# Reordered weight sums, later casts and value tiles transposed one at a time in a two-layer retention and convolution trunk

## The chip, the core and the metric

The kernel runs on one core of a Trainium2 chip. The core has TensorE (PE, matmuls, with PEld as its weight loads), VectorE (DVE), ScalarE (ACT), GpSimd (POOL) and SyncE (SP, which issues the DMAs here). Each engine takes its own instructions in the order of its own queue and waits for the others by semaphores. The metric is the device time of one execution in microseconds (us); it is given as the median of several runs, and one further execution was recorded by the profiler.

## The reference

A sequence of 528 tokens (16 learned ones and 512) with 1024 channels goes through two layers. A layer normalises its input, multiplies it by one large weight matrix, cuts the product into ten parts, and runs two branches on them:

```
xn = _rmsnorm(h, pre_norm_g[l])
proj = xn @ w_in[l] + b_in[l]
c_h, c_b, c_c, c_z, r_q, r_k, r_v, r_z, g_a, g_b = jnp.split(proj, split_at, axis=-1)
y_a = _short_conv_branch(c_h, c_b, c_c, c_z, conv_w[l], conv_b[l], w_conv_out[l])
y_b = _retention_branch(r_q, r_k, r_v, r_z, ret_gn_g[l], w_ret_out[l])
y = jax.nn.sigmoid(g_a) * y_a + jax.nn.sigmoid(g_b) * y_b
y = y @ w_o[l]
h = h + _rmsnorm(y, post_norm_g[l])
```

The convolution branch is a three-tap convolution over tokens of `c_c * c_h`, times `c_b` and `silu(c_z)`, times a weight matrix. The retention branch has 4 heads with 256 channels for q and k and 512 for v: q and k are rotated (rope), the scores q·k are weighted by a decay that is zero for keys of later chunks, the scores multiply v, each head's output is normalised over its 512 channels, multiplied by `silu(r_z)` and by a weight matrix. The chunkwise recurrence of the reference is computed here as one masked product per head. All is float32.

## The kernel before

**Matmuls in three products.** Every float32 operand is split into a high part (ACT's cast to float32r, L142) and a low part (DVE's subtraction, L143), by the helper `split`; a product is hi·hi + hi·lo + lo·hi, three matmuls. Weight pairs are called whi and wlo, and whd and wld for the fourth tile of a block; pairs of intermediate results are tiles of the ring r.

**Blocks of weights (`Group`).** A group is 256 output columns of the large matrix. It is computed by seven block products instead of eight, on sums of the input's blocks (A11 to S4 in Xh and Xl) and of the weight's blocks. Three raw weight tiles a, b, c of 128x1024 come by DMA into a ring of six (tag raw). DVE builds the weight sums in them: `halves(0)` adds the two halves of a and of c in place (L307, both here), then splits a; `sums` forms b's sum (L314) and t4 (L315) and splits b; `halves(2)` splits c; `last` splits t4. These four steps are queued by `prep` and carried out by `pump` whenever a pair of buffers comes free (four pairs, two single ones). A block product is one `mul`, 12 matmuls (four pieces of depth by three products) of up to 264 columns on PE (L279), followed by a `tick`. The results lie in PSUM banks pb (two), pc and pa (one each); `put` (L325, ACT) evicts them into SBUF slots with signs and biases, L335 copies one product into pa, and L356 (DVE) adds two results. `run` calls the callback cb of the group one block later.

**Side work (`later` and `tick`).** What follows from a block's result is not emitted at once: `later(delay, fn)` puts fn into a heap with the tick at which it is due, and `tick`, called after each `mul` and after every second step of the other matmul loops, runs what is due. So a delay is counted in block products of PE. The scheduler then places the instructions on each engine's queue; work under `tc.high_priority()` goes ahead of casts where both are ready.

**One retention head.** `k_done` and `q_done` call `rope`: two steps, each with two products (L403, L404), their sum or difference (L405) and a split into r tiles. `k8` (delay 3) copies a small piece of k twice. `scores` multiplies k and q (L422), DVE weights by the decay (L433), and a split writes Shi and Slo. `v_done` starts `vtrans`: the values, channel-major, are transposed on PE (L447) into token-major tiles, five key tiles of up to 128 keys (j = 0 to 4). Two of them share one `pslot`, a pp buffer of two PSUM banks; there are two pp buffers in all, which scores, attend, the statistics and the output products use too. For each key tile ACT writes the high part with the sum along the row (L454), then again with the mean taken off (L455; L459 for a piece of the last tile), and DVE writes the low part (L460). The sums `s` come from a ring of two (tag vs).

`z_done` runs when the gate z has arrived: silu on the second tile (L866), then `attend` for the four value pieces v = 0 to 3, two ticks apart: PE multiplies the scores by the values (L481) into the two banks of a pp (in layer 1 one bank); ACT squares a bank (L492), DVE multiplies the same bank by the norm's weight and the gate (L493), then the other bank in the same way; for v > 0 DVE adds the squares to `sums` (L496). `normed` follows: `stats` (L370 on PE reads `sums`), `wide` (a spread of the result), and `finish`, which multiplies by it (L514) and splits.

**Convolution and gates.** `conv_group` multiplies, convolves (L558, L562, L564) and gates (L568, L570, L574) in the callbacks of four groups; `gate_b` and `gate_a` apply the sigmoids. `RetOut` and `ConvOut` are the branch output products (L244 on PE), added into YB by L538 and L540.

**Opening.** The first head of each layer is computed by plain blocks (`Std`, L648) instead of groups, as the seven-product form needs sums of the input that aren't there yet; `with_r` (L992, L993) multiplies them by the token's norm, and L989 is their raw eviction.

Of the kernel before, what the change touches and what calls it, by code (L numbers as in the profile page):

```python
# [20 lines left out]
T = 528  # L21
# [35 lines left out]
def trunk(ctx: ExitStack, tc: tile.TileContext, xT, w_in, binT, w_co, w_ro, w_o, gpre, gpost,  # L57
# [226 lines left out]
    class Group:  # L284
        def __init__(self, l, col, i0, cb, act=AF.Identity):
            self.l, self.m, self.n, self.i0, self.cb, self.act = l, col // P, HALF - i0, i0, cb, act
            w = w_in[l, col // 256]
            need = [load(lambda j=j: self.load(j, w)) for j in range(3)][-1]
            prep("pair", need, 0, lambda: self.halves(0))
            prep("pair", need, 2, self.sums)  # L290
            prep("pair", need, 1, lambda: self.halves(2))
            prep("one", need, 0, self.last)
# [11 lines left out]
        def halves(self, j):  # L304
            if not j:
                for r in self.raw[0::2]:
                    nc.vector.tensor_tensor(r[:, 512:], r[:, 512:], r[:, 0:512], op=ALU.add)  # L307
            self.w[j] = wtile("whi"), wtile("wlo")
            split(*self.w[j], self.raw[j])
# [85 lines left out]
    def rope(tiles, t0):  # L395
# [5 lines left out]
        def step(u, v, op):  # L401
# [4 lines left out]
            hi, lo = rslot(), rslot()  # L406
            split(hi[:, cs], lo[:, cs], a[:, cs])
            res.append((hi, lo))
# [3 lines left out]
    def scores(l, q, k, k8, Shi, Slo, js):  # L412
# [14 lines left out]
        for n, j, cols in todo:  # L427
# [11 lines left out]
            split(Shi[0:kn, ss], Slo[0:kn, ss], sv)  # L439
# [23 lines left out]
    def attend(l, h, Shi, Slo, V, v, t, sums):  # L463
# [26 lines left out]
        with tc.high_priority():  # L490
            for b, (s0, s1) in enumerate(banks):
                nc.scalar.activation(sq[:, s0:s1], pp[:, b, 0:s1 - s0], AF.Square)  # L492
                nc.vector.scalar_tensor_tensor(t[:, s0:s1], pp[:, b, 0:s1 - s0], g, t[:, s0:s1], op0=ALU.mult, op1=ALU.mult)  # L493
# [6 lines left out]
    def normed(l, ts, sums, res):  # L500
# [11 lines left out]
        def finish(v):  # L512
            t = ts[v]
            nc.vector.tensor_tensor(t[:, cs], t[:, cs], st["rg"][:, cs], op=ALU.mult)  # L514
            hi, lo = rslot(), rslot()
            split(hi[:, cs], lo[:, cs], t[:, cs])
            res.append((hi, lo))
# [26 lines left out]
    def conv_group(l, i2, res):  # L544
# [7 lines left out]
        def c_c(ts):  # L552
            st["u"] = []
            for s in range(2):
                u = gr.tile([P, T + 2], F32, tag="u", name=nm("u"), bufs=2)
                if l < DEPTH - 1:
                    nc.vector.memset(u[:, 0:2], 0.0)
                nc.vector.tensor_tensor(u[:, 2 + cc.start:], ts[s][:, cc], st["h"][s][:, cc], op=ALU.mult)  # L558
                i = i2 * 2 + s
                a = ts[s]  # L560
                w = lambda j: cw_sb[:, l, j, i:i + 1]
                nc.scalar.activation(a[:, cs], u[:, 2 + cs.start:2 + T], AF.Identity, scale=w(2), bias=cb_sb[:, l, i:i + 1])  # L562
                for j in (1, 0):
                    nc.vector.scalar_tensor_tensor(a[:, cs], u[:, j + cs.start:j + T], w(j), a[:, cs], op0=ALU.mult, op1=ALU.add)  # L564
                st["u"].append(a)

        def c_z(ts):
            nc.scalar.activation(ts[1][:, cs], ts[1][:, cs], AF.Silu)  # L568
            for a, t in zip(st["u"], ts):
# [698 lines left out]
```

## Time and profile before

| | |
|---|---|
| median of 3 runs | 1588.45 us (1587.52 to 1591.75) |
| the profiled execution's own time | 1584.71 us |
| its span in the trace | 1582.9 us |
| PE busy | 1545.6 us, 98% |
| PEld busy | 1491.0 us, 94% |
| DVE busy | 1169.5 us, 74% |
| ACT busy | 909.7 us, 57% |
| POOL busy | 18.8 us, 1% |
| DMA moved | 174.37 MB, 110 GB/s on average |

The span is the time between the first and the last record of the trace. An engine is busy while it executes; waiting for a semaphore is idle time, which the trace ascribes to the instruction that came last of those waited for. The ends of matmuls are modelled, and matmuls overlap: a record lasts longer than the distance to the next one. PE and PEld run at the same time.

### The profile page before, as it was taken

The numbers are of one execution on the slowest core, as the hardware profiler recorded it, in microseconds if no ns is written. First come the engines' busy times: TensorE is split into PE (matmuls) and PEld (weight loads), VectorE is DVE, ScalarE is ACT, GpSimd is POOL, SyncE is SP. The second block draws the span as 40 slices with busy tenths as digits, with TensorE's granted clock in tenths as the row PEclk, the third lists the DMA queues.
The fourth block names the chain that finished last, engine by engine and source line by source line (L and its number), as shares of the span: only waits on it lengthen the run. The fifth ranks groups of instructions, "written<-read, shape, count | busy, mean of one in ns | idle before, by whom it ended". The sixth has DMA issues, their size and how long they took to land.

```text
span 1582.9 us, 29259 instructions
## 1 busy us (share of the span) xinstructions
PE 1545.6 (98%) x11762; PEld 1491.0 (94%) x11762; DVE 1169.5 (74%) x1702; ACT 909.7 (57%) x1763; POOL 18.8 (1%) x23
## 2 busy tenths in 40 slices
PE   9999999999999999999999999999999999999998
PEld 9988999999999999999999999999998999999986
DVE  6996776786877788867376878768869777997642
ACT  6584655555565466655354666665654655676531
POOL 0000000000000000000000000000000000000000
PEclk9999999999999999999999999999999999999999
DMA  8132322222232243335421223323232223334421
GB/s 266 61 114 71 116 101 94 94 101 87 101 107 94 89 139 127 126 129 187 122 102 48 101 86 115 114 94 114 94 107 101 94 88 131 130 130 141 144 94 53
DMA packets 86039, 174.37 MB, mean 110 GB/s; under 512 B 11280, under 2 KB 15888, under 8 KB 85904
## 3 DMA queue, kind: packets, MB, share of 16 engines
q1 hardware_dynamic: 85760, 172.50, 31.4%
q8 instruction: 92, 1.51, 0.4%
q14 instruction: 43, 0.35, 0.1%
q10 hardware_dynamic: 144, 0.01, 0.0%
HBM read 168.21 MB, written 4.26 MB: 109 GB/s over the span
## 4 chain that ended last, share of the span: by engine, by line
PE 81%; DVE 7%; ACT 6%; issue 3%; DMA 3%; SPq 0%; DVEq 0%; POOLq 0%; ACTq 0%
PE pb L279 26%; PE pp L244 16%; PE pc L279 13%; PE pp L648 7%; PE pa L279 7%; PE pp L481 4%; PE pp L1130 3%; PE pb L648 3%; DMA raw<-in_w_in 2%; DVE wlo L143 2%; ACT whi L142 2%; PE pp L422 2%; PE pp L384 1%; ACT r L454 1%; ACT r L455 1%
## 5 line engine op out<-in xcount | busy, mean ns | idle before, releaser
L143 DVE TENSOR_TENSOR wlo<-raw,whi 128x1024 fp32r<-128x1024 f32 (+2 forms) x358 | 392.9, 1107 | 140.7 <-ACT whi L142 138.3
L142 ACT CAST whi<-raw 128x1024 fp32r<-128x1024 f32 (+2 forms) x358 | 339.5, 958 | 235.1 <-PE pp L244 66.7
L279 PE MATMUL pb<-Xh,whi 128*128 128x264 f32 (+2 forms) x1008 | 289.4, 287 | 2.6 <-ACT pa L335 1.5
L279 PE MATMUL pb<-Xh,wlo 128*128 128x264 f32 (+2 forms) x1008 | 285.4, 283 | 0.1
L279 PE MATMUL pb<-Xl,whi 128*128 128x264 f32 (+2 forms) x1008 | 285.1, 283 | 0.0
L244 PE MATMUL pp<-r,whi 128*128 128x264 f32 (+1 forms) x1152 | 245.9, 321 | 0.0
L279 PE MATMUL pc<-Xh,whi 128*128 128x264 f32 (+2 forms) x672 | 193.7, 288 | 12.3 <-ACT f L325 12.2
L279 PEld LDWEIGHTS pb<-Xh,whi 128*128 128x128 f32 x1008 | 189.7, 188 | 4.8 <-ACT pa L335 2.1
L244 PEld LDWEIGHTS pp<-r,whi 128*128 128x128 f32 x1152 | 177.5, 188 | 15.9 <-ACT whi L142 0.5
L279 PE MATMUL pc<-Xl,whi 128*128 128x264 f32 (+2 forms) x672 | 191.0, 284 | 0.0
L279 PE MATMUL pc<-Xh,wlo 128*128 128x264 f32 (+2 forms) x672 | 190.7, 284 | 0.0
L279 PEld LDWEIGHTS pb<-Xl,whi 128*128 128x128 f32 x1008 | 189.7, 188 | 0.4
L279 PEld LDWEIGHTS pb<-Xh,wlo 128*128 128x128 f32 x1008 | 189.6, 188 | 0.4 <-DVE wlo L143 0.3
L244 PE MATMUL pp<-r,wlo 128*128 128x264 f32 (+1 forms) x576 | 152.8, 321 | 0.0
L307 DVE TENSOR_TENSOR raw<-raw 128x512 f32<-128x512 f32 x168 | 115.3, 686 | 43.6 <-DMA raw<-in_w_in 41.9
L279 PEld LDWEIGHTS pc<-Xh,whi 128*128 128x128 f32 x672 | 127.0, 189 | 16.3 <-ACT f L325 15.6
L279 PEld LDWEIGHTS pc<-Xl,whi 128*128 128x128 f32 x672 | 127.0, 189 | 0.2
L279 PEld LDWEIGHTS pc<-Xh,wlo 128*128 128x128 f32 x672 | 127.0, 189 | 0.1
L244 PEld LDWEIGHTS pp<-r,wlo 128*128 128x128 f32 x576 | 95.5, 188 | 8.0
L279 PE MATMUL pa<-Xh,whi 128*128 128x264 f32 (+2 forms) x336 | 96.7, 288 | 0.0
L279 PE MATMUL pb<-Xh,whd 128*128 128x264 f32 (+2 forms) x336 | 96.7, 288 | 0.0
L314 DVE TENSOR_TENSOR raw<-raw,raw 128x512 f32<-128x512 f32 x84 | 57.9, 689 | 51.8 <-DMA raw<-in_w_in 51.3
(219 smaller groups left out, 3329.6 us busy)
## 6 DMA issues: line engine op xcount, KB each, us to landing
raw<-in_w_in SPq DMA_DIRECT2D x426, 256.0 KB, 2.9
raw<-in_w_ro SPq DMA_DIRECT2D x32, 512.0 KB, 3.2
raw<-in_w_in SPq DMA_DIRECT2D x20, 512.0 KB, 5.0
raw<-in_w_co SPq DMA_DIRECT2D x16, 512.0 KB, 3.2
raw<-in_w_o SPq DMA_DIRECT2D x16, 512.0 KB, 3.6
Dsb<-in_decay SPq DMA_DIRECT2D x8, 520.0 KB, 4.7
h1d<-f SPq DMA_DIRECT2D x8, 264.0 KB, 4.4
f<-h1d SPq DMA_DIRECT2D x8, 264.0 KB, 4.3
```

The costliest lines, as they stand in the source:

```text
L142: nc.scalar.copy(dst_hi, src)
L143: nc.vector.tensor_tensor(dst_lo, src, dst_hi.bitcast(F32), op=ALU.subtract)
L244: nc.tensor.matmul(banks[i][:, 0:cols.n], wt(k)[:, msl], xs(k)[:, sl], start=(k == 0 and a == 0), stop=(k == nk - 1 and a == 2),)
L279: nc.tensor.matmul(o[:, 0:n], wt[:, k, :], xs[:, blk, k, HALF - n:], start=(first and k == 0 and a == 0), stop=(k == 3 and a == 2), skip_g ...
L307: nc.vector.tensor_tensor(r[:, 512:], r[:, 512:], r[:, 0:512], op=ALU.add)
L314: nc.vector.tensor_tensor(b[:, 0:512], a[:, 512:], c[:, 0:512], op=ALU.add)
L384: nc.tensor.matmul(pp[:, c // per, (c % per) * sc:(c % per + 1) * sc], y[:, c:c + 1].to_broadcast([sc, P]), ident[0:sc, 0:sc], start=True, ...
L422: nc.tensor.matmul(pp[0:kn, n + i, 0:cols.n], k[dt][x][:, k0:k0 + kn] if j < 4 else k8[:, dt * 2 + x, :], q[dt][y][:, sl], start=(dt == 0 ...
L454: nc.scalar.activation(hi[0:kn], pv, AF.Copy, scale=-1.0 / DV, accum_out=s)
L481: nc.tensor.matmul(pp[:, b, lo_ - banks[b][0]:hi_ - banks[b][0]], V[j][x][0:kn, v * P:(v + 1) * P], S[0:kn, SOFF[j] + lo_ - q0:SOFF[j] + h ...
L648: nc.tensor.matmul(o, wt(k), xs[:, i0:], start=(k == 0 and a == 0), stop=(k == KD - 1 and a == 2))
L1130: nc.tensor.matmul(o, x[:, xs], wo[k][half][w], start=(k == 0 and a == 0), stop=(k == KD - 1 and a == 2))
```

## The change

The instructions are the same and as many. Six things are emitted in another place:

- the sum in the third weight tile c (L307) is made in `halves(2)`, when c is split, and no longer in `halves(0)`; `halves(0)` now asks for the load of a alone;
- casts that follow products of DVE are put into `later`: those of `rope` by two ticks, those of `scores` and `finish` by one, `k8` from 3 to 5; `finish` itself begins at 14 in place of 15;
- the pieces of `conv_group`, and the silu and sigmoid of z and of the gates, are spread over zero to three ticks;
- in `attend` the squares of both banks come first, then both products;
- `vtrans` is called for one key tile at a time, every two ticks, and each has a pp buffer of its own (five in place of three per head);
- `v_done` starts three ticks earlier (34 to 31, 16 to 13, 12 to 9).

```
-            need = [load(lambda j=j: self.load(j, w)) for j in range(3)][-1]
-            prep("pair", need, 0, lambda: self.halves(0))
-            prep("pair", need, 2, self.sums)
-            prep("pair", need, 1, lambda: self.halves(2))
-            prep("one", need, 0, self.last)
+            need = [load(lambda j=j: self.load(j, w)) for j in (0, 1, 2)]
+            prep("pair", need[0], 0, lambda: self.halves(0))
+            prep("pair", need[2], 2, self.sums)
+            prep("pair", need[2], 1, lambda: self.halves(2))
+            prep("one", need[2], 0, self.last)
...
         def halves(self, j):
-            if not j:
-                for r in self.raw[0::2]:
-                    nc.vector.tensor_tensor(r[:, 512:], r[:, 512:], r[:, 0:512], op=ALU.add)
+            if j != 1:
+                r = self.raw[j]
+                nc.vector.tensor_tensor(r[:, 512:], r[:, 512:], r[:, 0:512], op=ALU.add)
...
             nc.vector.tensor_tensor(a[:, cs], a[:, cs], b[:, cs], op=op)
-            hi, lo = rslot(), rslot()
-            split(hi[:, cs], lo[:, cs], a[:, cs])
-            res.append((hi, lo))
+
+            def halves():
+                hi, lo = rslot(), rslot()
+                split(hi[:, cs], lo[:, cs], a[:, cs])
+                res.append((hi, lo))
+            later(2, halves)
...
-            split(Shi[0:kn, ss], Slo[0:kn, ss], sv)
+            later(1, lambda kn=kn, ss=ss, sv=sv: split(Shi[0:kn, ss], Slo[0:kn, ss], sv))
...
                 nc.scalar.activation(sq[:, s0:s1], pp[:, b, 0:s1 - s0], AF.Square)
+            for b, (s0, s1) in enumerate(banks):
                 nc.vector.scalar_tensor_tensor(t[:, s0:s1], pp[:, b, 0:s1 - s0], g, t[:, s0:s1], op0=ALU.mult, op1=ALU.mult)
...
             nc.vector.tensor_tensor(t[:, cs], t[:, cs], st["rg"][:, cs], op=ALU.mult)
-            hi, lo = rslot(), rslot()
-            split(hi[:, cs], lo[:, cs], t[:, cs])
-            res.append((hi, lo))
+
+            def halves():
+                hi, lo = rslot(), rslot()
+                split(hi[:, cs], lo[:, cs], t[:, cs])
+                res.append((hi, lo))
+            later(1, halves)
...
+            for s in range(2):
+                later(1 + s, lambda s=s: last_tap(s))
+                later(2 + s, lambda s=s: taps(s))
...
+            later(1, silu)
+            later(1, lambda: gate(0))
+            later(2, lambda: gate(1))
...
+            for s in range(2):
+                later(s, lambda s=s: product(s))
+                later(1 + s, lambda s=s: halves(s))
...
-            later(3, k8)
+            later(5, k8)
...
-                for n, js in enumerate(((0, 1), (2, 3), (4,))):
-                    later(d + 3 * n, lambda js=js: vtrans(vt, hd["v8"], V, js))
+                for j in range(len(JT)):
+                    later(d + 2 * j, lambda j=j: vtrans(vt, hd["v8"], V, (j,)))
...
-                nc.scalar.activation(ts[n][:, cs], ts[n][:, cs], AF.Silu)
+                later(1, lambda n=n: nc.scalar.activation(ts[n][:, cs], ts[n][:, cs], AF.Silu))
...
             for v in range(4):
-                later(15 + v, lambda v=v: hd["n"][2](v))
+                later(14 + v, lambda v=v: hd["n"][2](v))
...
-                add(Group(l, R_V + h * DV + n * 256, I_ALL[l], lambda ts, d=d: v_done(ts, d, 34)))
+                add(Group(l, R_V + h * DV + n * 256, I_ALL[l], lambda ts, d=d: v_done(ts, d, 31)))
...
-    v_done(vt, hd["hd"], 16)
+    v_done(vt, hd["hd"], 13)
...
-            v_done(opened[2:6], hd["hd"], 12)
+            v_done(opened[2:6], hd["hd"], 9)
```

The line numbers of the changed kernel differ: the value tile's steps L447, L454, L455, L459 and L460 are L450, L457, L458, L462 and L463 there, attend's L481, L492, L493 and L496 are L484, L495, L497 and L500, the decay's L433 is L436 and the add into YB is L547.

Below stand instructions in the order of one engine's queue; the numbers behind the tiles' names tell buffers apart and mean nothing else.

ACT before, in head 1 of layer 0, from the third value tile (L454 into r_2895) to the copy into pa (the tiles pp_2981 and pp_3049 hold the transposed values, pc_2930 and pb_2929 two block products, whi the casts of weights):

```order
L454 ACTIVATE r_2895,vs_2990<-pp_2981 128x512
L455 ACTIVATE r_2895<-pp_2981,vs_2990 128x512
L325 ACTIVATE f_2928<-pb_2929 128x264
L454 ACTIVATE r_2897,vs_2994<-pp_2981 128x512
L142 CAST whi_3026<-raw_2657 128x1024
L455 ACTIVATE r_2897<-pp_2981,vs_2994 128x512
L325 ACTIVATE f_2926<-pa_108 128x264
L454 ACTIVATE r_2899,vs_3054<-pp_3049 128x512
L142 CAST whi_3075<-raw_2798 128x1024
L455 ACTIVATE r_2899<-pp_3049,vs_3054 128x512
L459 ACTIVATE r_2900<-pp_3049,vs_3054 64x512
L325 ACTIVATE f_2927<-pc_2930,bin_92 128x264
```

ACT in the changed kernel at the same place, from the fourth value tile (pp_2992) on; pp_3028 holds the fifth, pc_2932 and pb_2931 the block products:

```order
L457 ACTIVATE r_2823,vs_2997<-pp_2992 128x512
L458 ACTIVATE r_2823<-pp_2992,vs_2997 128x512
L325 ACTIVATE f_2930<-pb_2931 128x264
L142 CAST whi_3040<-raw_2659 128x1024
L457 ACTIVATE r_2825,vs_3033<-pp_3028 128x512
L458 ACTIVATE r_2825<-pp_3028,vs_3033 128x512
L462 ACTIVATE r_2826<-pp_3028,vs_3033 64x512
L325 ACTIVATE f_2928<-pa_108 128x264
L325 ACTIVATE f_2929<-pc_2932,bin_92 128x264
L142 CAST whi_3078<-raw_2800 128x1024
L325 ACTIVATE f_2929<-pb_2931,bin_92 128x264
L335 ACTIVATE pa_108<-pb_3086,bin_92 128x264
```

Each value tile now has a pp of its own and its two or three ACT steps stand together; between the fifth tile's steps and the eviction of pc_2932 there is no cast of weights any more, and the next cast comes behind that eviction.

DVE before, at the beginning of the same head's transposed values (r_2892 is the low part of the first tile, r_2894 of the second):

```order
L314 TENSOR_TENSOR raw_2801<-raw_2798,raw_2859 128x512
L307 TENSOR_TENSOR raw_2859<-raw_2859 128x512
L143 TENSOR_TENSOR wlo_2922<-raw_2561,whi_2921 128x1024
L356 TENSOR_TENSOR f_2740<-f_2740,f_2741 128x528
L460 SCALAR_TENSOR_TENSOR r_2892<-pp_2901,vs_2910,r_2891 80x512
L143 TENSOR_TENSOR wlo_2961<-raw_2564,whi_2960 128x1024
L460 SCALAR_TENSOR_TENSOR r_2894<-pp_2901,vs_2914,r_2893 128x512
L143 TENSOR_TENSOR wld_3034<-t_2957,whd_3033 128x512
L307 TENSOR_TENSOR raw_2964<-raw_2964 128x512
L460 SCALAR_TENSOR_TENSOR r_2896<-pp_2981,vs_2990,r_2895 128x512
L315 TENSOR_TENSOR t_3111<-raw_2801 128x512
```

DVE in the changed kernel (r_2818 is the low part of the first tile, r_2820 of the second):

```order
L463 SCALAR_TENSOR_TENSOR r_2818<-pp_2827,vs_2832,r_2817 80x512
L143 TENSOR_TENSOR wlo_2873<-raw_2495,whi_2872 128x1024
L436 TENSOR_TENSOR f_2866<-pp_2853,Dsb 128x192
L436 TENSOR_TENSOR f_2868<-pp_2853,Dsb 128x64
L143 TENSOR_TENSOR Slo_2631<-f_2866,Shi_2630 128x192
L143 TENSOR_TENSOR Slo_2631<-f_2868,Shi_2630 128x64
L314 TENSOR_TENSOR raw_2803<-raw_2800,raw_2876 128x512
L307 TENSOR_TENSOR raw_2876<-raw_2876 128x512
L463 SCALAR_TENSOR_TENSOR r_2820<-pp_2895,vs_2900,r_2819 128x512
L143 TENSOR_TENSOR wlo_2924<-raw_2562,whi_2923 128x1024
L356 TENSOR_TENSOR f_2739<-f_2739,f_2740 128x528
```

The first tile's low part has moved from behind the weight sums L314 and L307 and a weight's low half to ahead of them; the second tile's stands behind the two sums in both.

DVE before, at a rope of k (f_3892 and f_3913 are its two results, r_3898 and r_3919 their low parts, YB the accumulated branch output):

```order
L403 TENSOR_TENSOR f_3892<-f_3757,cos_sb 128x528
L540 TENSOR_TENSOR YB<-pp_3879,YB 128x528
L404 TENSOR_TENSOR f_3893<-f_3758,sin_sb 128x528
L405 TENSOR_TENSOR f_3892<-f_3892,f_3893 128x528
L540 TENSOR_TENSOR YB<-pp_3923,YB 128x528
L143 TENSOR_TENSOR r_3898<-f_3892,r_3897 128x528
L143 TENSOR_TENSOR wlo_3953<-raw_3596,whi_3952 128x1024
L403 TENSOR_TENSOR f_3913<-f_3757,sin_sb 128x528
L540 TENSOR_TENSOR YB<-pp_3963,YB 128x528
L404 TENSOR_TENSOR f_3914<-f_3758,cos_sb 128x528
L405 TENSOR_TENSOR f_3913<-f_3913,f_3914 128x528
L314 TENSOR_TENSOR raw_3863<-raw_3860,raw_3956 128x512
```

DVE in the changed kernel (f_3895 and f_3912, r_3935 and r_3951):

```order
L403 TENSOR_TENSOR f_3895<-f_3761,cos_sb 128x528
L547 TENSOR_TENSOR YB<-pp_3882,YB 128x528
L404 TENSOR_TENSOR f_3896<-f_3762,sin_sb 128x528
L403 TENSOR_TENSOR f_3912<-f_3761,sin_sb 128x528
L405 TENSOR_TENSOR f_3895<-f_3895,f_3896 128x528
L404 TENSOR_TENSOR f_3913<-f_3762,cos_sb 128x528
L547 TENSOR_TENSOR YB<-pp_3918,YB 128x528
L405 TENSOR_TENSOR f_3912<-f_3912,f_3913 128x528
L143 TENSOR_TENSOR r_3935<-f_3895,r_3934 128x528
L143 TENSOR_TENSOR wlo_3957<-raw_3599,whi_3956 128x1024
L547 TENSOR_TENSOR YB<-pp_3967,YB 128x528
L143 TENSOR_TENSOR r_3951<-f_3912,r_3950 128x528
```

The products and sums of both steps now stand together, ahead of both low parts and of the weight's low half; the second sum has passed one add into YB and the low half wlo.

## Rows read from the trace of the kernel before

**Rows 1.** Page, part 1: busy time, share of the span, instructions of each engine.

```profile
PE 1545.6 (98%) x11762; PEld 1491.0 (94%) x11762; DVE 1169.5 (74%) x1702; ACT 909.7 (57%) x1763; POOL 18.8 (1%) x23
```

**Rows 2.** PE's waits, whole kernel: line and releaser, us in total, times, longest.

```profile
PE pc L279 <- ACT f L325: 12.2, 13, 1.6
PE pp L370 <- DVE f L496: 4.8, 3, 3.6
...
PE pp L481 <- DVE r L460: 1.6, 3, 0.7
PE pb L279 <- ACT pa L335: 1.5, 3, 0.6
...
PE pb L648 <- ACT f L989: 1.2, 1, 1.2
PE pb L279 <- ACT f L989: 1.1, 1, 1.1
```

**Rows 3.** Timeline, vtrans of head 1: start, duration, engine, line; in brackets idle before.

```profile
232.01 1.04 PE L447 MATMUL pp<-ident,f 128*80 128x128 f32 x8
233.74 0.69 DVE L314 TENSOR_TENSOR raw<-raw,raw 128x512 f32<-128x512 f32 x1 [1.73 <-DMA raw<-in_w_in]
235.23 0.69 DVE L307 TENSOR_TENSOR raw<-raw 128x512 f32<-128x512 f32 x1 [0.80 <-DMA raw<-in_w_in]
237.60 0.74 DVE L460 SCALAR_TENSOR_TENSOR r<-pp,vs,r 80x512 fp32r<-80x512 f32 x1
238.38 0.60 ACT L454 ACTIVATE r<-pp 128x512 fp32r<-128x512 f32 x1
...
248.34 0.68 ACT L459 ACTIVATE r<-pp,vs 64x512 fp32r<-64x512 f32 x1
248.90 0.48 ACT L325 ACTIVATE f<-pc,bin 128x264 f32<-128x264 f32 x1
249.44 0.40 PE L279 MATMUL pc<-Xh,whi 128*128 128x264 f32 x1 [1.02 <-ACT f L325]
249.67 0.28 PE L279 MATMUL pc<-Xl,whi 128*128 128x264 f32 x1
249.79 0.29 PE L279 MATMUL pc<-Xh,wlo 128*128 128x264 f32 x1
```

**Rows 4.** PE's waits in the stretch from 160 to 165 us.

```profile
PE pc L279 <- ACT f L325: 0.7, 1, 0.7
```

**Rows 5.** Busy us (instructions) of PE, PEld, DVE, ACT, POOL; granted clock; DMA share, GB/s.

```profile
141.00:147.70 6.70, 5.71 (x30) 5.74 (x31) 3.94 (x8) 3.19 (x7) 1.71 (x1) 0.50 0.11 39
...
250.00:253.60 3.60, 3.60 (x19) 3.60 (x18) 2.51 (x4) 1.67 (x4) 0.00 (x0) 0.53 0.48 151
253.60:258.00 4.40, 4.40 (x36) 4.32 (x35) 2.63 (x4) 1.99 (x5) 0.00 (x0) 1.00 0.32 119
```

**Rows 6.** Timeline, the last attend (v = 3) of head 0 in layer 0.

```profile
139.14 0.69 DVE L307 TENSOR_TENSOR raw<-raw 128x512 f32<-128x512 f32 x1 [1.66 <-DMA raw<-in_w_in]
...
140.21 0.44 ACT L492 ACTIVATE f<-pp 128x320 f32<-128x320 f32 x1 [3.23 <-DVE f L493]
...
140.68 0.55 DVE L493 SCALAR_TENSOR_TENSOR f<-pp,gn_sb,f 128x320 f32<-128x320 f32 x1 [0.51 <-ACT f L492]
...
141.99 0.42 PE L370 MATMUL pp<-ones_d,f 128*88 128x1 f32 x2 [3.65 <-DVE f L496]
```

**Rows 7.** Waits of ACT and DVE, whole kernel.

```profile
ACT f L492 <- DVE f L493: 24.2, 15, 3.9
...
DVE raw L314 <- DMA raw<-in_w_in: 51.3, 43, 2.6
DVE raw L307 <- DMA raw<-in_w_in: 41.9, 36, 3.6
```

**Rows 8.** Timeline, a rope of k and the scores behind it.

```profile
330.44 0.63 ACT L142 CAST r<-f 128x528 fp32r<-128x528 f32 x1 [3.94 <-DVE f L405]
...
333.21 0.71 PE L422 MATMUL pp<-r,r 128*80 128x264 f32 x4 [0.63 <-DVE r L143]
```

More of the change, by code (lines that the diff above doesn't have):

```diff
@@ L552, in c_c @@
         def c_c(ts):
-            st["u"] = []
+            st["u"] = [t for t in ts]
+            us = []
+            w = lambda s, j: cw_sb[:, l, j, i2 * 2 + s:i2 * 2 + s + 1]
             for s in range(2):
                 u = gr.tile([P, T + 2], F32, tag="u", name=nm("u"), bufs=2)
+                us.append(u)
                 if l < DEPTH - 1:
@@ L558, in c_c, with last_tap, taps @@
                 nc.vector.tensor_tensor(u[:, 2 + cc.start:], ts[s][:, cc], st["h"][s][:, cc], op=ALU.mult)
-                i = i2 * 2 + s
+            def last_tap(s):
+                nc.scalar.activation(ts[s][:, cs], us[s][:, 2 + cs.start:2 + T], AF.Identity, scale=w(s, 2),
+                                     bias=cb_sb[:, l, i2 * 2 + s:i2 * 2 + s + 1])
+            def taps(s):
                 a = ts[s]
-                w = lambda j: cw_sb[:, l, j, i:i + 1]
-                nc.scalar.activation(a[:, cs], u[:, 2 + cs.start:2 + T], AF.Identity, scale=w(2), bias=cb_sb[:, l, i:i + 1])
@@ L563, in c_c @@
                 for j in (1, 0):
-                    nc.vector.scalar_tensor_tensor(a[:, cs], u[:, j + cs.start:j + T], w(j), a[:, cs], op0=ALU.mult, op1=ALU.add)
-                st["u"].append(a)
-        def c_z(ts):
-            nc.scalar.activation(ts[1][:, cs], ts[1][:, cs], AF.Silu)
-            for a, t in zip(st["u"], ts):
-                nc.vector.tensor_tensor(a[:, cs], t[:, cs], a[:, cs], op=ALU.mult)
+                    nc.vector.scalar_tensor_tensor(a[:, cs], us[s][:, j + cs.start:j + T], w(s, j), a[:, cs],
+                                                   op0=ALU.mult, op1=ALU.add)
@@ new lines, in c_c, with silu, gate @@
+            for s in range(2):
+                later(1 + s, lambda s=s: last_tap(s))
+                later(2 + s, lambda s=s: taps(s))
+        def c_z(ts):
+            def silu():
+                nc.scalar.activation(ts[1][:, cs], ts[1][:, cs], AF.Silu)
+            def gate(s):
+                a = st["u"][s]
+                nc.vector.tensor_tensor(a[:, cs], ts[s][:, cs], a[:, cs], op=ALU.mult)
+            later(1, silu)
+            later(1, lambda: gate(0))
+            later(2, lambda: gate(1))
@@ L572, in c_b, with product, halves @@
         def c_b(ts):
-            for a, t in zip(st["u"], ts):
-                nc.vector.tensor_tensor(t[:, cs], t[:, cs], a[:, cs], op=ALU.mult)
+            def product(s):
+                nc.vector.tensor_tensor(ts[s][:, cs], ts[s][:, cs], st["u"][s][:, cs], op=ALU.mult)
+            def halves(s):
                 hi, lo = rslot(), rslot()
-                split(hi[:, cs], lo[:, cs], t[:, cs])
+                split(hi[:, cs], lo[:, cs], ts[s][:, cs])
                 res.append((hi, lo))
+            for s in range(2):
+                later(s, lambda s=s: product(s))
+                later(1 + s, lambda s=s: halves(s))
@@ L913, in gate_b, with sigmoid, times @@
             cs = slice(QCOLS[l].t0, T)
-            nc.scalar.activation(ts[1][:, cs], ts[1][:, cs], AF.Sigmoid)
-            for s, t in enumerate(ts):
+            def sigmoid():
+                nc.scalar.activation(ts[1][:, cs], ts[1][:, cs], AF.Sigmoid)
+            def times(s):
                 y = YB[:, b * 2 + s, cs]
-                nc.vector.tensor_tensor(y, y, t[:, cs], op=ALU.mult)
+                nc.vector.tensor_tensor(y, y, ts[s][:, cs], op=ALU.mult)
+            later(0, lambda: times(0))
+            later(1, sigmoid)
+            later(2, lambda: times(1))
         for b in range(4):
@@ L924, in gate_a @@
             cs = slice(QCOLS[l].t0, T)
-            nc.scalar.activation(ts[1][:, cs], ts[1][:, cs], AF.Sigmoid)
+            later(1, lambda: nc.scalar.activation(ts[1][:, cs], ts[1][:, cs], AF.Sigmoid))
             ga.extend(ts)
```

## Prediction

> **What bounds the kernel now.** I read the page's head first. TensorE (PE) is busy for 1545.6 of 1582.9 us, 98% [rows 1]; VectorE (DVE) has 74% and ScalarE (ACT) 57%. So DVE and ACT matter only where PE stands still for them, and everything that this change can give lies in PE's 37.3 us of idle time and in the stretches where its clock is low. No edit takes an instruction away; each only reorders.
>
> The second view is PE's list of waits [rows 2]: who ended PE's idle time, the total, how often, the longest. The reader is to see that one kind rules: matmuls into pc (bank c of the next block, its S1 product) wait for the eviction of pc on ACT (L325), 13 times, 12.2 us. Next is L370, the statistics matmul behind attend, for DVE's L496: 3 times, 4.8 us. Then L481 (attend) for L460 (the last step of a transposed value tile), 1.6 us; the pa copy L335, 1.5; two waits of the opening for L989, 1.2 and 1.1.
>
> A gap costs a little more than it shows. A matmul's record lasts 0.28 us, but the next one starts 0.12 us after it [rows 3], at 249.67 and 249.79, so each stop adds about 0.16 us to its gap.
>
> The third view is the timeline around single gaps: what stands in front of the late instruction on its own queue.
>
> **Where the pc waits come from: vtrans.** In [rows 3] two value tiles share one pp buffer. ACT's L454 for the second tile waits until DVE's L460 has read the first. DVE stood in front of DMA waits (1.73 us before L314 and 0.80 before L307), so L460 of the tile transposed at 232.01 ran only at 237.60, and ACT's next L454 at 238.38. All evictions queue behind it on ACT. Eight us later the same thing ends in PE's gap of 1.02 us at 249.44: L325 of pc runs at 248.90, behind a cast and the value steps, the last of them L459 at 248.34. Eleven of the thirteen pc waits are of this kind, by what stands on ACT in front of them; the other two, of which [rows 4] has one (0.7 us), follow finish's casts, in each layer one. So vtrans costs 12.2 − 1.4 + 1.6 = 12.4 us in 14 gaps (three of them L481's), and 14 × 0.16 = 2.2 on top: **14.6 us**.
>
> **The clock.** After 249.44 the granted clock is 0.53 for 3.60 us, in which 19 matmuls ran [rows 5]; at full clock 36 took 4.40 us, 0.122 each, so 19 need 2.3 and the dip cost 1.3 us. After the attend gap of 3.65 us it is 0.50: 30 matmuls in 5.71 us instead of 3.7, so **2.0 us** more.
>
> **The change part by part.**
>
> *One key tile per pp, earlier (vtrans).* Five pp buffers a head in place of three, same transposes, same ACT and DVE instructions. What goes is the wait of ACT for DVE inside a pp: the order shows each L457 waiting for its own transposes only. The last tile also comes three ticks earlier relative to the products that need it, a tick being one mul of 12 matmuls, 12 × 0.122 = 1.46 us, so L460's lateness at attend (0.7 us at the longest) [rows 2] is covered by more than four. And pc's eviction stands ahead of the whi cast that was before it. I take 13.0 of the 14.6, since some heads will still meet an eviction behind two value steps (L457 and L458 take 0.6 to 0.7 us each), and 1.0 of the 1.3 us of clock: **−14.0**. Bounds: 0, and −15.9.
>
> *Both squares ahead of both products (attend).* Before, the second bank's square waited for the first bank's product on DVE, and the second product for that square. In [rows 6], for v=3: L307 waits for its DMA until 139.14, product one follows it, square two comes only at 140.21 (ACT stood 3.23 us for the product), product two at 140.68 after 0.51 us, then L496, and PE goes on at 141.99. Over the kernel ACT's wait there is 24.2 us [rows 7]. After, DVE's 0.51 us is gone for each v. It adds up only where one v's products delay the next: here each of four v has such a step of about 0.5 us on DVE, and DVE's wlo between them sets free the raw buffer whose load the next L307 waits for. The chain would be 4 × 0.5 = 2.0 us earlier; I take 1.9. If the load does not follow, it is 0.5 to 1.0. The other two gaps on L370 are 4.8 − 3.6 = 1.2 us with 0.3 for their starts: about 1.4 in all, each under 0.85, which half a microsecond and an earlier chain should close: −1.4. The clock's 2.0 us at the first one go if the shorter gap keeps the clock up; I take half, −1.0. **−4.3**, between −0.5 and −7.3.
>
> [...] The rows show 0.50 after a gap of 3.65 us, and 0.53 after gaps of 0.7 and 1.02 us close together [rows 2, 3, 5, 6]. [...]
>
> *Rope's casts two ticks later, k8 at 5.* PE's L422 at 333.21 waits 0.63 us for DVE's cast of k, and ACT's cast at 330.44 stood 3.94 us for L405 [rows 8]. The order now has both rope products ahead of the casts and of an add into YB; with the third pa wait (1.5 − 2 × 0.6 = 0.3 us, at the pa copy behind the same casts) and the starts of both there is 1.3 us: **−1.3**, bounds 0 and that. Delaying a cast puts it nearer to the scores that read it; with L422 now behind both ropes, that is the price if I am wrong, up to the same 1.3.
>
> *The opening (with_r, ropes of head 0).* The two waits for L989 are 2.3 us [rows 2] and 0.3 for starting. Evictions stand further ahead on ACT there, yet PE has fewer pc muls to fill in: **−1.8**, bounds 0 and −2.6.
>
> *Finish's casts one tick later, begun one earlier.* The order around the gap of [rows 4] stays cast of whi, cast of r, eviction: **0**, bounds −3.3 (both pc gaps and two of L335 of 0.6, with starts) and +0.5 a head.
>
> *Conv and gate pieces, the z silu, the scores' casts.* No conv or gate line stands among PE's releasers [rows 2], so PE hides them; they cost nothing as long as PE's queue there has no wait. Same cost in instructions.
>
> *The weight sums.* L307 of the third weight tile moves from ahead of the first tile's cast to ahead of its own. DVE executes as many. L307 waits 41.9 us for DMA and L314 51.3 [rows 7]; the wait moves from the one to the other, because L314 reads that third tile in any case. What gains is the first tile's lo half, no longer queued behind the third tile's load; PE hardly ever waits for wlo, so **0**.
>
> *What the new order costs.* The order has 39 transposes that wait for a pp buffer instead of 24, and 19 evictions that wait for DVE to leave a slot instead of 9. The nearest rows are stops of PE of 0.16 us and up. 15 and 10 more at about 0.1 each: **+2.5**, between 0 and the slower rival's price.
>
> **Sum.** −14.0 − 4.3 − 1.3 − 1.8 + 2.5 = −18.9 us. The profiled execution took 1584.71 us, 3.74 under the median of 1588.45. So 1565.8 in its place, and about **1570 us** as a median.
>
> **Rivals.**
>
> *Half of it (DMA stays ahead on DVE).* DVE's 93 us of DMA waits [rows 7] stand in front of L463, L356 and L497 in the new order too. Then the ACT queue still waits for DVE, at the silu behind L356 for one, and half of each gain is lost: −7.0 − 2.1 − 0.7 − 0.9 + 1.0 = −9.7, **1578.7**. For it: in [rows 6] the load, not the square, sets 139.14. Against: in [rows 3] the tile's L460 stands behind L314 and L307, and the new order puts the first of them ahead.
>
> *The gaps only move.* The evictions stay behind other casts, and the gap of one product appears at the next: the change does not do what it says. −2 to 0, **1587**. Against: most gaps have free time behind them on ACT (57% busy).
>
> *Slower: pp buffers run out.* There are two pp buffers, and five tiles a head now pass through them, two muls (2.9 us) apart, so a buffer must be free 5.8 us after its transposes. In [rows 3] the first was transposed at 232.01 and let go at 238.34 (L460 of 0.74 us at 237.60): 6.3 us. If DVE lets go as late in the new order, PE stands at the transposes in place of pc, in order, with everything behind it. One DMA wait (up to 2.6 us [rows 7]) a head: 8 × 2.5 = 20 us, and vtrans gains nothing: 20 − 4.3 − 1.3 − 1.8 = +12.6, **1601**. It decides where the release passes 5.8 us; 0.5 us less and it costs nothing. Against: L463 of the first tile now precedes both waits.
>
> **Chances.** Forecast 0.60, half 0.24, moved 0.10, slower 0.06. About 0.3% (4.8 us) is what a measurement of this kernel can tell from no change. Faster than 1583.7: 0.60 + most of 0.24 = 0.82; within: 0.12; slower than 1593.2: 0.06. The range of 8 in 10 goes from 1561 (all gaps and clock gone, with half of the new costs) to 1584 (the half case with its own spread); left out are the moved and the slower case and a little at the fast end.
>
> **What would show it.** Right: pc's row for L325 falls from 12.2 to under 3 us, L481's row for L460 vanishes, ACT's wait for the product is gone, L370's row falls under 2.5, and the granted clock near 250 us stays at full. Half: the pc row between 4 and 9, with L463 or L356 behind L314 and L307. Moved: PE's idle time near 35 us under other names. Slower: a row of transposes (L450) that wait for L463, above 8 us. I should be wrong most easily in the new order's cost, which no row of before shows.

## The result, and the profile after

The changed kernel took 1564.61 us as a median (1560.22 to 1567.43, 4 runs) against 1588.12 us before: 23.5 us less, ratio 0.9845 with a 95% interval of 0.9817 to 0.9873. A second measurement, with the experiments below, gave 0.9832 (0.9811 to 0.9853). The forecast was 1570 with a range of 1561 to 1584: the time lies in the range, 5.4 us under the forecast. How the gain came about was only partly forecast: the largest term came out in size, but not by the cause that was given for it.

The page of the changed kernel's profiled execution, part 1 (before: [rows 1]):

```profile
span 1558.4 us, 29296 instructions
...
PE 1537.1 (99%) x11762; PEld 1487.0 (95%) x11762; DVE 1166.1 (75%) x1702; ACT 912.2 (59%) x1763; POOL 18.8 (1%) x23
```

PE's idle time is 21.3 us in place of 37.3, with as many matmuls. PE's waits, whole kernel (line and releaser, us in total, times, longest; before: [rows 2]):

```profile
PE pb L279 <- ACT pa L335: 2.3, 4, 0.8
...
PE pp L370 <- DVE f L500: 1.7, 2, 1.5
PE pc L279 <- ACT f L325: 1.5, 2, 0.7
...
PE pb L279 <- ACT f L1026: 1.1, 1, 1.1
```

The pc row is down from 12.2 us to 1.5, and those two are the stops behind finish's casts that [rows 4] showed. The row of attend for the last value tile (1.6 us) is gone. L370's is down from 4.8 to 1.7, L1026 is one wait instead of L989's two.

In DVE's and PE's timeline the last attend of head 0 reads thus (before: [rows 6]):

```profile
135.72 0.69 DVE L307 TENSOR_TENSOR raw<-raw 128x512 f32<-128x512 f32 x1 [1.65 <-DMA raw<-in_w_in]
136.34 0.89 DVE L497 SCALAR_TENSOR_TENSOR f<-pp,gn_sb,f 128x208 f32<-128x208 f32 x2
137.14 0.70 DVE L500 TENSOR_TENSOR f<-f,f 128x528 f32<-128x528 f32 x1
...
137.98 0.60 PE L370 MATMUL pp<-ones_d,f 128*88 128x1 f32 x6 [1.50 <-DVE f L500]
```

Both products now run together (x2), with no wait for a square between them. L307 still waits 1.65 us for its load in front of them, and 1.50 us of PE's stop are left. The granted clock after it and near 240 us (busy us and instructions of PE, PEld, DVE, ACT, POOL; clock; DMA share, GB/s; before: [rows 5]):

```profile
138.00:142.00 4.00, 4.00 (x37) 4.00 (x38) 3.24 (x6) 1.34 (x2) 1.66 (x1) 1.00 0.18 66
236.00:240.00 4.00, 3.96 (x32) 3.74 (x32) 3.31 (x5) 3.97 (x9) 0.00 (x0) 1.00 0.26 91
```

It is 1.00 in both stretches; before it was 0.50 and 0.53.

To add this up I took from both traces the distance of each matmul's start to the next one's and subtracted the usual distance of that shape in the kernel before. What is over 0.25 us is a stop. Matmuls in stretches of low granted clock have a row of their own.

| between the first and the last matmul, us | before | after |
|---|---|---|
| usual distances | 1512.3 | 1512.3 |
| stops over 0.25 us | 36.1 (35) | 18.1 (22) |
| extra at the low clock | 4.2 | 0.0 |
| extra of 0.04 to 0.25 us and the rest | 22.9 | 20.6 |

So of 24.5 us, 18.0 are stops, 4.2 the clock, and 2.3 delays too small to count as stops.

### The profile page after: what moved, and what is told of

Its sections match the earlier page's. It is cut to its first block, busy times and chain, and to the rows that moved or that the text cites. A ratio compares the mean times of both kernels' runs of the same rounds, so it can differ in the third digit from the quotient of the medians.

```text
span 1558.4 us, 29296 instructions
## 1 busy us (share of the span) xinstructions
PE 1537.1 (99%) x11762; PEld 1487.0 (95%) x11762; DVE 1166.1 (75%) x1702; ACT 912.2 (59%) x1763; POOL 18.8 (1%) x23
## 4 chain that ended last, share of the span: by engine, by line
PE 91%; DVE 4%; ACT 2%; DMA 1%; issue 1%; SPq 0%; DVEq 0%; POOLq 0%; ACTq 0%
PE pb L279 29%; PE pp L244 18%; PE pc L279 15%; PE pa L279 7%; PE pp L678 7%; PE pp L484 4%; PE pb L678 3%; PE pp L1167 3%; PE pp L425 2%; DMA raw<-in_w_in 1%; PE pp L450 1%; DVE wlo L143 1%; PE pp L384 1%; PE pp L370 1%; ACT whi L142 1%
## 5 line engine op out<-in xcount | busy, mean ns | idle before, releaser
L307 DVE TENSOR_TENSOR raw<-raw 128x512 f32<-128x512 f32 x168 | 115.3, 688 | 27.8 <-DMA raw<-in_w_in 27.0
L314 DVE TENSOR_TENSOR raw<-raw,raw 128x512 f32<-128x512 f32 x84 | 58.0, 690 | 57.6 <-DMA raw<-in_w_in 57.4
```

The lines of the kernel that those rows point to most:

```text
L314: nc.vector.tensor_tensor(b[:, 0:512], a[:, 512:], c[:, 0:512], op=ALU.add)
```

## The experiments

Times are ratios to the kernel before, run in turn with it on the same chip, with their 95% intervals. The kernel before had medians of 1590.2 to 1591.1 us in these sessions. "Stops" are those of the table above in each kernel's profiled execution; one execution of the same kernel can differ from the next by about 3 us in them (the changed kernel had 18.1 and 21.2).

| kernel | ratio | median us | stops us | pc row us | L370 row us |
|---|---|---|---|---|---|
| before | | 1590.4 | 36.1 | 12.2 | 4.8 |
| changed, again | 0.9832 (0.9811 to 0.9853) | 1563.7 | 21.2 | 2.6 | 2.1 |
| vtrans' part alone | 0.9924 (0.9902 to 0.9945) | 1577.0 | 27.1 | 2.9 | 5.7 |
| early start alone | 0.9905 (0.9885 to 0.9925) | 1575.4 | 24.8 | 3.4 | 4.2 |
| all but vtrans' part | 0.9932 (0.9912 to 0.9952) | 1580.0 | 31.8 | 12.2 | 1.5 |
| all but the split into tiles | 0.9838 (0.9815 to 0.9860) | 1564.2 | 17.8 | 2.2 | 1.6 |
| all, heads 1 to 3 at the old start | 0.9863 (0.9843 to 0.9883) | 1568.2 | 21.7 | 4.8 | 1.8 |
| attend's part alone | 0.9963 (0.9949 to 0.9976) | 1584.5 | 36.0 | 13.7 | 1.1 |
| all but attend's part | 0.9863 (0.9845 to 0.9881) | 1569.3 | 22.0 | 2.1 | 4.6 |
| moved sums alone | 1.0008 (0.9995 to 1.0021) | 1591.8 | 39.7 | 12.7 | 4.8 |
| all but the moved sums | 0.9851 (0.9831 to 0.9871) | 1566.0 | 22.1 | 4.2 | 1.8 |
| later casts alone | 0.9972 (0.9961 to 0.9984) | 1585.2 | 35.8 | 11.6 | 4.8 |
| changed, statistics one tick later | 0.9834 (0.9814 to 0.9854) | 1562.8 | 17.4 | 2.2 | none |

**The changed kernel again.** No edit.

> The changed kernel once more, as the measure for the runs beside it. My theory: 1560 to 1567 us, where the time within that goes with the mean granted clock of the execution (1.000 gave 1560.2, 0.997 gave 1563.9, 0.995 gave 1567.4): about 1.4 us per 0.001. Rival: the spread has another cause, and executions of equal clock differ by more than 3 us.

It gave 1563.1 to 1564.3 us at mean clocks of 0.998 to 1.000. Over the 49 executions of the kernel before in these sessions, time and mean granted clock go together (correlation −0.80, 1.6 us per 0.001); within each of the twelve kernels of this section, 77 executions, it is 1.2 us per 0.001. So the clock goes with a good part of the spread, near the slope that was expected. But executions of equal clock still differ, the kernel before by up to 4.6 us within one session (1590.67 and 1595.23 at 0.993), the changed kernel by 4.1 us between the two measurements (1560.22 and 1564.34, both at 1.000), so the rival has a part too.

**vtrans' part alone, and all but it.** The edit, on the kernel before and taken back from the changed one (with the starts 16 and 12 of head 0 becoming 13 and 9):

```
-                for n, js in enumerate(((0, 1), (2, 3), (4,))):
-                    later(d + 3 * n, lambda js=js: vtrans(vt, hd["v8"], V, js))
+                for j in range(len(JT)):
+                    later(d + 2 * j, lambda j=j: vtrans(vt, hd["v8"], V, (j,)))
...
-                add(Group(l, R_V + h * DV + n * 256, I_ALL[l], lambda ts, d=d: v_done(ts, d, 34)))
+                add(Group(l, R_V + h * DV + n * 256, I_ALL[l], lambda ts, d=d: v_done(ts, d, 31)))
```

> The kernel before with one part of the change alone: one key tile per pp buffer in vtrans, begun three ticks earlier. Theory (the vtrans stops are the bulk and go by this edit alone): about 14 us less than before, 1574, and PE's row pc L279 <- ACT f L325 falls from 12.2 to about 2 us. Rival (DVE's DMA waits hold the chain unless the sums and casts move too): half, 1581, the pc row at 5 us or more.

> The changed kernel with vtrans as before (two key tiles per pp, old start). Theory: it gives back 14 us, 1578, with about ten pc waits on L325. Rival (the other edits carry part of what went): 1570, the pc row at 5 us or less.

Alone it gave about 12 us by its ratio (13 by medians), and the pc row fell to 2.9; without it 16 us by medians came back, with 14 pc waits of 12.2 us. The bulk of the gain hangs on this part, and the moved DMA waits are no condition of it: half of it, as the rival had it, would have left 5 us or more in the pc row.

**Only the split taken back.** The changed kernel with pairs of tiles, but with the start at 31:

```
-                for j in range(len(JT)):
-                    later(d + 2 * j, lambda j=j: vtrans(vt, hd["v8"], V, (j,)))
+                for n, js in enumerate(((0, 1), (2, 3), (4,))):
+                    later(d + 3 * n, lambda js=js: vtrans(vt, hd["v8"], V, js))
```

> The changed kernel with two key tiles per pp, but begun three ticks earlier as in the changed one: it separates the early start from the split. Theory (ACT's wait for DVE inside a pp holds the evictions whenever it begins; the early start only saves attend's waits for the last tile, 2.1 us): about 1576. Rival (the early start is what counts, since only the tile before attend was late): 1566.

It gave 1564.2 us, as the changed kernel. My theory said 1576 and fell: begun early, tiles may share a pp buffer without a loss. PE's waits there:

```profile
PE pb L279 <- ACT pa L335: 2.3, 4, 0.8
PE pc L279 <- ACT f L325: 2.2, 4, 0.8
```

So I formed another one from the timelines. ACT's queue in head 1 of the kernel before, between the shared tiles and the late eviction of [rows 3]:

```profile
237.71 0.65 ACT L866 ACTIVATE f<-f 128x528 f32<-128x528 f32 x1 [2.58 <-DVE f L356]
...
241.63 0.61 ACT L454 ACTIVATE r<-pp 128x512 fp32r<-128x512 f32 x1
...
243.88 0.60 ACT L454 ACTIVATE r<-pp 128x512 fp32r<-128x512 f32 x1 [0.54 <-DVE r L460]
244.46 1.04 ACT L142 CAST whi<-raw 128x1024 fp32r<-128x1024 f32 x1
...
246.25 0.61 ACT L454 ACTIVATE r<-pp 128x512 fp32r<-128x512 f32 x1
...
246.82 1.06 ACT L142 CAST whi<-raw 128x1024 fp32r<-128x1024 f32 x1
```

ACT stands 2.58 us before L866, the silu of z. That waits for L356 on DVE, which stands behind the two DMA waits of [rows 3]. Of the head's five tiles four still come after that point, with their casts and evictions, and from 243.88 on ACT never stands again until pc's eviction at 248.90: a backlog. The wait for L460 inside a pp shows as 0.54 us of all that, and as 5.0 us of ACT's time in the whole kernel. More of it may be hidden: the second tile's L454 at 238.38 starts as both the silu (238.36) and the first tile's L460 (238.34, [rows 3]) end, for L460 stands directly behind L356 on DVE. It is so in all six of these heads, and the trace can't tell which of the two held that tile. In the trace of before four tiles come after L866 in each of heads 1 to 3 of both layers, six heads in all; with the start three ticks earlier it is two, in each of the six.

**The early start alone, and the split alone.** Two kernels that tell this theory from the first. The kernel before with nothing but

```
-                add(Group(l, R_V + h * DV + n * 256, I_ALL[l], lambda ts, d=d: v_done(ts, d, 34)))
+                add(Group(l, R_V + h * DV + n * 256, I_ALL[l], lambda ts, d=d: v_done(ts, d, 31)))
...
-    v_done(vt, hd["hd"], 16)
+    v_done(vt, hd["hd"], 13)
...
-            v_done(opened[2:6], hd["hd"], 12)
+            v_done(opened[2:6], hd["hd"], 9)
```

> The kernel before with nothing but vtrans begun three ticks earlier, two key tiles per pp as they were. Theory A, formed after the run with pairs begun early (the place counts: in the last muls before attend ACT has the last value tiles, casts of weights and the evictions to do at once, so pc's eviction comes late; sharing a pp does no harm): about 1577, as one tile per pp begun early, the row pc L279 <- ACT f L325 at 4 us or less. Theory B, mine of the prediction (ACT's wait for DVE inside a shared pp): 1588, that row at 10 us or more.

and the changed kernel with one tile per pp, but heads 1 to 3 started as before:

```
-                add(Group(l, R_V + h * DV + n * 256, I_ALL[l], lambda ts, d=d: v_done(ts, d, 31)))
+                add(Group(l, R_V + h * DV + n * 256, I_ALL[l], lambda ts, d=d: v_done(ts, d, 34)))
```

> The changed kernel with one key tile per pp, but heads 1 to 3 of both layers begun at 34 as before (head 0 keeps the new start). Theory B (a pp of its own is what helps): 1564, the pc row under 2.5 us. Theory A (the place counts): stops come back at several of the six heads, 1570 or more, the pc row at 5 us or more.

The early start alone gave 1575.4 us, all that vtrans' part gave alone (1577.0). ACT's timeline at the same place:

```profile
236.41 0.65 ACT L866 ACTIVATE f<-f 128x528 f32<-128x528 f32 x1 [1.22 <-DVE f L356]
237.07 0.60 ACT L454 ACTIVATE r<-pp 128x512 fp32r<-128x512 f32 x1
...
240.33 0.61 ACT L454 ACTIVATE r<-pp 128x512 fp32r<-128x512 f32 x1
...
243.53 0.49 ACT L325 ACTIVATE f<-pc,bin 128x264 f32<-128x264 f32 x1
```

Two tiles come after the silu. The eviction of pc at 243.53 stands behind the last tile's steps, one cast of weights and one eviction, and PE has no stop there. The fourth tile's L454 at 237.07 again starts as both the silu (237.06) and the third tile's L460 (237.04) end, and here that costs nothing. PE's rows:

```profile
PE pp L370 <- DVE f L496: 4.2, 3, 2.9
PE pc L279 <- ACT f L325: 3.4, 5, 1.3
```

The split without the early start gave 1568.2 us, against 1580.0 with neither and 1564.2 with the early start instead:

```profile
PE pc L279 <- ACT f L325: 4.8, 8, 0.8
```

That is between the two theories: four tiles come after the silu again, waits of pc are back in heads 1 to 3, but they are fewer and shorter than in the kernel with neither. ACT in head 1, where L896 is the silu:

```profile
233.52 0.65 ACT L896 ACTIVATE f<-f 128x528 f32<-128x528 f32 x1 [2.29 <-DVE f L356]
...
241.58 0.48 ACT L325 ACTIVATE f<-pc,bin 128x264 f32<-128x264 f32 x1
...
244.15 0.61 ACT L457 ACTIVATE r<-pp 128x512 fp32r<-128x512 f32 x1
```

In the kernel with neither, PE's matmul into pc is late 10.4 to 11.7 us after the start of the silu in each of the six heads, and 4.1 us after it in three of them. Here the late stops are gone in all six, and stops of 0.20 to 0.83 us stand 4.1 us after it in five. The eviction of pc that the late stops waited for now passes ahead of the fifth tile (241.58 and 244.15; in the kernel before 248.90 and 246.25), in all six. So here too it counts what stands ahead of an eviction; whether the tile's own pp or its later tick (d + 8 in place of d + 6) let it pass, no run shows.

So either edit alone takes away most; the early start takes nearly all, and the split adds nothing measurable to it. What the split does by itself (12 us against neither, of which head 0's start is a part) was not taken apart further.

**attend's part alone, and all but it.**

```
                 nc.scalar.activation(sq[:, s0:s1], pp[:, b, 0:s1 - s0], AF.Square)
+            for b, (s0, s1) in enumerate(banks):
                 nc.vector.scalar_tensor_tensor(t[:, s0:s1], pp[:, b, 0:s1 - s0], g, t[:, s0:s1], op0=ALU.mult, op1=ALU.mult)
```

> The kernel before with one part of the change alone: in attend both squares ahead of both products. Theory: PE's row L370 <- L496 falls from 4.8 us to about 2, with the granted clock of the first dip kept or not: 3 to 5 us less than before, 1584. Rival (the DMA load in front of the last L307 does not come earlier): under 1 us less, 1587.5, and the gap at head 0 stays above 3 us.

> The changed kernel with attend as before (square and product in turn for each bank). Theory: it gives back 3 to 5 us, 1568, with a gap of 3 us or more before L370 of head 0. Rival (the earlier vtrans and the moved sums make the gap short by themselves): 1565, the gap under 2 us.

5.9 us alone by its ratio, 5.5 us given back by medians: up to one more than expected at most. L370's row goes with it both times (4.8 to 1.1, and 4.6 without, of which 3.3 are at head 0). DVE's timeline with attend's part alone, where L494 and L497 are its product and sum, with PE's row:

```profile
138.16 0.69 DVE L307 TENSOR_TENSOR raw<-raw 128x512 f32<-128x512 f32 x1 [1.54 <-DMA raw<-in_w_in]
138.76 0.89 DVE L494 SCALAR_TENSOR_TENSOR f<-pp,gn_sb,f 128x208 f32<-128x208 f32 x2
...
140.41 1.07 PE L370 MATMUL pp<-ones_d,f 128*88 128x1 f32 x12 [1.10 <-DVE f L497]
```

PE's stop begins at 138.34 in the kernel before and at 139.31 here (the start of L370 less its gap). Against that point the last L307, which its load holds up, starts 0.80 us later before and 1.15 us earlier here: the load comes about 2 us earlier, as the chain of the prediction needs. The stop fell from 3.65 to 1.10 us. In this profiled execution as many stops elsewhere stood against it (36.0 us in all), and the timed runs alone show the gain.

**The moved sums alone, and all but them.** The `prep` lines of the change go with it.

```
-            if not j:
-                for r in self.raw[0::2]:
-                    nc.vector.tensor_tensor(r[:, 512:], r[:, 512:], r[:, 0:512], op=ALU.add)
+            if j != 1:
+                r = self.raw[j]
+                nc.vector.tensor_tensor(r[:, 512:], r[:, 512:], r[:, 0:512], op=ALU.add)
```

> The kernel before with one part of the change alone: the sum of the third weight tile made when that tile is split. Theory: DVE's DMA waits move from L307 to L314, no effect on PE: 1588, within 2 us. Rival (DVE comes sooner to what PE waits for): 4 us or more less, 1584.

> The changed kernel with both sums of a block made when its first tile is split, as before. Theory: 1565, as the changed one, within 2 us. Rival (the third tile's load in front of casts and value tiles on DVE brings stops back): 1569 or more.

Alone the interval includes no change. Taken back, the kernel was 2.3 us slower by medians, and the intervals (0.9851 against 0.9832) overlap: an effect can't be told from none. The DMA waits did not move from L307 to L314 as forecast. With the sums moved alone L307 waits 39.3 us in place of 41.9, and L314 67.7 in place of 51.3. In the changed kernel L307 waits 27.0 us where it waits 48.2 with the sums taken back, and L314 57.4 where it waits 58.2.

**The later casts alone.** The changed kernel with vtrans, attend and the sums as before.

> The kernel before with the casts and gate pieces put later alone (rope, k8, scores, finish, convolution, gates, silu of z); vtrans, attend and weight sums as before. Theory: the rope's stops go (1.6 us) and a little at the opening, 1588, with the pc row of vtrans still at 11 us or more. Rival (the later casts clear ACT and DVE in front of the value tiles too): 1582, the pc row under 8.

4.5 us by its ratio, between the two expectations; the pc row stays at 11.6, so the casts don't clear the way for the value tiles. In its profiled execution PE's time without the low clock is 1.4 us under that of the kernel before; the rest of the 4.5 us isn't shown by that trace. Nor is it the clock: its mean was 0.9952 in these runs and 0.9948 in those of the kernel before beside them, some 0.6 us. It stays open.

**The statistics one tick later**, an attempt to beat the changed kernel:

```
-            later(10, lambda: hd["n"][0]())
+            later(11, lambda: hd["n"][0]())
```

> The changed kernel with the statistics matmul of attend one tick later (11 in place of 10): PE has one more block product to do while DVE adds the last squares. Theory: the two stops of L370 (1.5 and 0.2 us of idle) go and nothing else moves: about 2 us under the changed kernel, 1562. Rival (the chain behind it, the power on GpSimd, the spread, finish's casts, comes later and stops PE there): 1565 or more, with a stop at L384 or L425 or larger ones at finish's casts.

L370's stops are gone. The time, 0.9834 against 0.9832, is the same. Its trace has three small stops of pc in heads 1 and 3 (0.61, 0.41 and 0.30 us) where the changed kernel has one, and a larger one at 718 us (0.97 against 0.51). That would be most of the 2.0 us won at L370. But the second trace of the changed kernel has such stops too (0.85, 0.51 and 0.44 us in head 2), so it isn't shown that the later statistics brought them.

## Why the prediction was right, and where not

Its terms, against the stops of the two traces (each gap with its start, as in the prediction):

| term | forecast us | in the traces us |
|---|---|---|
| vtrans, stops | −13.0 | −13.8 |
| attend, stops | −3.3 | −3.2 |
| clock | −2.0 | −4.2 |
| rope | −1.3 | −1.6 |
| opening | −1.8 | −0.4 |
| finish | 0 | 0.0 |
| new stops | +2.5 | +1.2 |
| small delays | not named | −2.3 |
| sum | −18.9 | −24.3 |

*vtrans.* The step that failed is "What goes is the wait of ACT for DVE inside a pp". With pairs kept and the start moved the gain was the same, both alone (1575.4 against 1577.0 us) and in the changed kernel (1564.2 against 1563.7): that wait need not go. I had credited the early start with attend's waits alone, a seventh of the term. What holds by the runs is the place: vtrans begins early enough that two and not four of its tiles fall behind the point where ACT stands for DVE. The size was read from the right rows, but that it came out, −13.8 us against −13.0, is luck as far as the cause goes: the early start, in the same edit, took away the stops that I gave to the pp buffers. That the standing at the silu is what makes the backlog is read from the timelines. No run took the silu's wait away by itself, and in the kernel before the wait inside a pp ends at the same moment. A slip in reading besides: the gap at 249.44 comes eleven us after 238.38, not eight.

*attend.* Right in mechanism and, for the stops, in size: the stop at head 0 lost 2.1 us (3.65 to 1.50), where 1.9 was forecast.

*The clock.* The forecast took half of the first dip and most of the second; both went. But this term can't be read from two traces. A dip did not follow from a stop alone here. The same stop of 1.71 us at the layer's boundary stands in both of the following (and in the kernel before at 810 us, with the clock at 1.00). The changed kernel, timeline and stretch:

```profile
793.40 0.51 PE L678 MATMUL pb<-Xh,whi 128*128 128x264 f32 x2 [1.71 <-ACT Xh L142]
```

```profile
793.00:801.00 8.00, 7.60 (x64) 7.60 (x65) 6.65 (x18) 3.21 (x9) 0.97 (x1) 1.00 0.47 162
```

and the kernel with the split taken back:

```profile
793.51 0.79 PE L678 MATMUL pb<-Xh,whi 128*128 128x264 f32 x2 [1.71 <-ACT Xh L142]
```

```profile
793.60:800.40 6.80, 6.80 (x33) 6.80 (x34) 5.61 (x17) 2.77 (x7) 0.97 (x1) 0.50 0.57 178
```

In the one the clock stays at 1.00, in the other it is at half for 6.8 us, in which PE did 33 matmuls. The mean granted clock over timed runs is the better measure: 0.9946 in 49 runs before, 0.9985 in 4 of the changed kernel (0.9973 in its first 4), which at 1.6 us per 0.001 is 4 to 6 us, an estimate. Over the thirteen kernels of the table the mean clock is the higher the fewer the stops are (correlation −0.83). So fewer stops went with a higher mean clock here, and by that estimate the clock's share is about a fifth of the gain, at least twice what I gave it. The two stretches show only that the same stop was followed by a dip in one and not in the other; what decides it, no run shows.

*The opening.* One of the two waits went (L989 at 76.59), one stayed. ACT and PE there in the changed kernel:

```profile
81.83 1.28 ACT L1030 ACT_TABLE_LOAD   x1
83.12 0.74 ACT L1030 ACTIVATE f<-f,bin 128x528 f32<-128x528 f32 x1
83.77 0.64 ACT L1026 COPY f<-pb 128x264 f32<-128x264 f32 x2
...
84.17 0.39 PE L279 MATMUL pb<-Xh,whi 128*128 128x264 f32 x1 [1.15 <-ACT f L1026]
...
89.08 0.39 PE L279 MATMUL pb<-Xh,whi 128*128 128x264 f32 x1 [0.77 <-ACT pa L335]
```

In the kernel before ACT had

```profile
81.55 1.28 ACT L993 ACT_TABLE_LOAD   x1
...
85.69 0.36 ACT L989 COPY f<-pb 128x264 f32<-128x264 f32 x1
```

So the load of a table, 1.28 us, stood in front of this eviction in both. A cast of weights that came between the two is gone from there, and L1026 comes 1.92 us earlier than L989 did. But PE gets to this point as much earlier (its stop begins at 83.02 in place of 84.97), and the stop is as long (1.15 us against 1.1). The prediction names this price, that "PE has fewer pc muls to fill in", and set it too low. Together with a new stop of pa at 89.08 the opening gained 0.4 us.

*The rivals.* The half case saw rightly that the DMA waits stay (84.4 against 93.2 us in sum) and that the silu behind L356 holds ACT (14.7 us at L896 in the changed kernel, 15.0 at L866 before); but with two tiles and not four behind that point the pc row is 1.5 us in place of 12.2. The slower case did not come: no transpose (L450) is among PE's waits, whose smallest row is 0.2 us. The new costs were half of what I allowed, and not of the kinds that were counted: a wait for a weight's low half at 14 us (0.40), and evictions behind ACT's own work at 622 and 718 us (0.28 and 0.51).

*What adds up.* The parts alone give 12.1, 5.9, −1.3 and 4.5 us, together 21.2, the whole 26.7 by its ratio of 0.9832. With intervals of 2 to 3 us on each, a gain from the parts' company can neither be shown nor excluded.

## What to carry to other kernels

When one engine's late answer stops another, look for where its queue last stood still and count what came after: moving work ahead of that point can pay even where the waits inside that work stay, as pairs begun earlier gave what single tiles did (1564.2 against 1563.7 us). Where two waits end at the same moment, a trace names one of them, and only an edit that takes one away can tell them apart. Split a combined edit by experiment before crediting its more visible half; the delay constants carried what I gave to the buffers. A gain that comes with fewer stops of TensorE should be measured over several executions with their granted clocks, which differed here from one to the next (0.992 to 0.997 in 49 executions of the kernel before).

## What was not expected of the hardware

The granted clock was 0.50 for 6.8 us after a stop of PE of 1.71 us in the trace of the changed kernel with the split taken back, and 1.00 after the same stop in the traces of the changed kernel and of the kernel before. Its mean differed between executions of the same program (0.992 to 0.997 in 49 of the kernel before), and time went with it by about 1.2 to 1.6 us of 1590 for each 0.001. Together with the run to run spread of the kernel before (1586.1 to 1595.2 us over 11 runs in one session) that is the noise against which parts of 2 us can't be told from nothing here.
